# Both products of each rotation in the S5 scan on the vector engine, in a two-layer hybrid trunk on one Trainium2 core

## The chip, the core and the metric

The kernel runs on one core of one Trainium2 chip. The metric is device time in microseconds, from the first to the last instruction of one launch, of the median of the runs. Before the change it is 2625.96 us (three runs, 2624.56 to 2633.85 us). The engines are named as the profile names them: PE is the tensor engine (PEld its weight loads), DVE the vector engine, ACT the scalar engine, POOL is GpSimd, SP issues the weight loads.

## What is computed

Two layers of a decoder trunk for 256 tokens of width 2048. Layer 0 projects the normalised input once (2048 x 4632) and feeds two mixers, an S5 complex-diagonal state space (512 channels in 32 groups of 16, 64 complex states per group) and a Mamba-2 SSD mixer; layer 1 feeds an RWKV-7 mixer and an RG-LRU in the same manner. Each layer ends with an output projection, a squared-ReLU MLP (2048 to 8192 and back) and a gated embedding; a last RMSNorm ends the program. All is float32. The part that matters here is the scan of S5:

```python
bu_re = jnp.einsum('bsgh,gph->bsgp', ug, bbar_re)
bu_im = jnp.einsum('bsgh,gph->bsgp', ug, bbar_im)
def combine(e1, e2):
    a1r, a1i, b1r, b1i = e1
    a2r, a2i, b2r, b2i = e2
    return (a2r * a1r - a2i * a1i, a2r * a1i + a2i * a1r,
            a2r * b1r - a2i * b1i + b2r, a2r * b1i + a2i * b1r + b2i)
_, _, xr, xi = lax.associative_scan(combine, (a_re, a_im, bu_re, bu_im), axis=1)
y = einsum('ghp,bsgp->bsgh', c_re, xr) - einsum('ghp,bsgp->bsgh', c_im, xi)
```

## The kernel before

Weights stream from memory in tiles of 512 KB (128 x 1024 values, `raw`), three in flight. Each tile is split into a high part `wh` (an ACT copy, line 172) and a low part `wl` (a DVE subtraction, line 153), three buffers of each in layer 0, and PE makes three passes with them: `gemm_as` (lines 339 to 341, 512 columns at a time) and `gemm_ws` (lines 358 to 360, 256 columns). A tile feeds PE with 12 products of 512 columns or 24 of 256. So PE can't go on without the next `wl`, and neither ACT nor DVE can split further ahead than the three buffers that PE gives back.

Layer 0 (`even`) goes through a list of steps, `ORA`, in which S0 to S3 are the four tiles of S5 (`s5_tile`, 128 channels each), T the tables of cos and sin, U the loads of u, Z, C, B and X0 pieces of the big projection with their convolutions on DVE (line 166, `c<-fpad`), Q scores, and E the decays of the SSD mixer (`ssd_decays`, lines 843 to 876: softplus, sums by PE, exponentials, the transposes on line 868, and after them the exponents on lines 901 and 902). The list `ORB` follows with the SSD groups.

The complex recurrence is made real: the inputs are rotated by the angle of each state back to a common phase, two real scans run, and the result is rotated forth. One `s5_tile` holds four such pieces j of 32 channels. For each piece PE makes the two inputs (line 667) into PSUM, ACT copies them to SBUF as `b` (128 x 512), `s5_rotate` turns them (sign -1), DVE scans two chunks of 128 tokens with a carry between them (line 681, the carry `kar` by ACT and DVE), `s5_rotate` turns the states (sign 1), and PE multiplies them with C (line 685). So there are 4 x 4 x 2 = 32 rotations. A rotation has two products with broadcast tables, `p2` with sin and `p1` with cos, 128 x 512 each, and two sums of halves, 128 x 256 each. The helpers are `tt` (line 153, on `self.ve`, which is DVE here) and `gtt` (line 156, always POOL).

The program is written through a tile framework whose scheduler lays out one fixed order for each engine, from its own estimate of each instruction's cost. At run time each engine works through its own order and waits on semaphores for the others. High-priority parts (the weight splits) are put ahead where the scheduler can.

Of the kernel before, what the change touches and what calls it, by code (L numbers as in the profile page):

```python
# [15 lines left out]
OP = mybir.AluOpType  # L16
PSUM = bass.MemoryType.PSUM
# [6 lines left out]
S5C = 128  # L24
S5N = 16
# [31 lines left out]
# order of the steps of layer 0 (to the S5 part, and after it) and of layer 1; see even() and odd()  # L57
# [4 lines left out]
# steps that go first when their inputs are there, and steps of layer 0 whose weights are not split ahead  # L62
URGENT = ("G1", "Q")
LATE_W = ("L", "Pa01", "X0")
# steps of layer 1 whose weights are split ahead, and projections in column blocks of 256
EARLY_W = ("D2", "D3", "L00", "L01", "L10", "L11")
N256 = ("D0", "D3")
# column blocks of the embedding gate
# [3 lines left out]
class K:  # L72
# [20 lines left out]
    @contextmanager  # L93
    def on_pool(self, on=True):
        """Small elementwise work goes to GpSimd."""
        if on:
            self.ve = self.nc.gpsimd
        yield
        self.ve = self.nc.vector
# [4 lines left out]
    @contextmanager  # L104
    def phase(self, name, wp, **n):
        """Buffers of split weights and PSUM banks of a phase: accumulators, transposes, and others by tag."""
        with ExitStack() as st:
            if wp:
                self.wp = st.enter_context(self.weights(name, wp))
            self.ps = st.enter_context(self.tc.tile_pool(name="ps" + name, bufs=1, reuse_waits="tile", space=PSUM))  # L110
            self.nb = n
            yield
# [165 lines left out]
    def rsqrt_small(self, v, n):  # L278
        """Exponent halving, a fitted step (to 7e-4) and one of third order."""
        b = self.small(n, I32)  # L280
        self.ts(b, v.bitcast(I32), 1, None, OP.logical_shift_right)
        y = self.small(n)
        self.ts(y.bitcast(I32), b, -1.0, 1595932665.0, OP.mult, OP.add)
        w, q = self.small(n), self.small(n)
        k = 0.703952253 * 3 / 8
        self.tt(w, y, y, OP.mult)
        self.stt(w, w, -k, v, OP.mult, OP.mult)
        self.stt(y, w, 2.38924456 * k, y, OP.add, OP.mult)
        self.stt(w, y, 64.0 / 9, y, OP.mult, OP.mult)
        self.tt(w, w, v, OP.mult)  # L290
        self.stt(q, w, -10.0 / 3, w, OP.add, OP.mult)
        self.stt(y, q, 5.0, y, OP.add, OP.mult)
        return y

# [27 lines left out]
    def gemm_as(self, xs, W, r0, c0, nn=512, shared=False):  # L322
        """x times columns of W, tokens on partitions: an accumulator per 128 tokens, or both in one bank."""
        nk = len(xs)
        if shared:
            q = self.acc([128, 2, nn])
            ps = [q[:, 0], q[:, 1]]
        else:
            ps = [self.acc([128, nn]) for _ in range(2)]
        step = 2 * 512 // nn  # L330
        f = dict(skip_group_check=True)
        for kb in range(0, nk, step):
            wh, wl = self.wtile(W, r0[kb] if isinstance(r0, list) else r0 + kb, step, c0, nn)
            for kk in range(step):
                k = kb + kk
                h, l = xs[k]
                for t in range(2):
                    s = slice(128 * t, 128 * t + 128)
                    self.nc.tensor.matmul(ps[t], h[:, s], wh[:, kk], start=k == 0 and not (shared and t), stop=False, **f)  # L339
                    self.nc.tensor.matmul(ps[t], h[:, s], wl[:, kk], start=False, stop=False, **f)  # L340
                    self.nc.tensor.matmul(ps[t], l[:, s], wh[:, kk], start=False, stop=k == nk - 1, **f)  # L341
        return ps
# [21 lines left out]
    def prep(self, src, g, j0, nj, alloc=None):  # L364
        """src(t, j): [128 tokens, 128] of feature tile j; g(j): per-feature scale or None."""
        hb, lb = ((alloc or self.t4)([128, nj, T], FR) for _ in range(2))
        for i in range(nj):
            q = self.pq([128, T])
            for t in range(2):
                self.nc.tensor.transpose(q[:, 128 * t:128 * t + 128], src(t, j0 + i), self.ident)  # L370
            if g is None:
                self.split(hb[:, i], lb[:, i], q)
            else:
                s = g(j0 + i)
                self.pa = self.act(hb[:, i], q, AF.Copy, scale=s)
                self.pv = self.stt(lb[:, i], q, s, hb[:, i].bitcast(F32), OP.mult, OP.subtract)
                self.pas.append((self.pa, self.pv))
        return [(hb[:, i], lb[:, i]) for i in range(nj)]

    def norm_prep(self, gname):  # L380
        """Transposed, scaled and split h, and the reciprocal rms of each token."""
        xs = []
        ss = self.small(8)
        last = []
# [24 lines left out]
    def load_x(self, src, W, pool):  # L409
        """The input and the first weights, in the order of their use."""  # L410
        self.h = [[self.c([128, 1024], pool=pool) for _ in range(2)] for _ in range(2)]
        self.early = []
        for b in range(4):
            for t in range(2):
                self.nc.sync.dma_start(self.hv(t, 512 * b, 512), src[128 * t:128 * t + 128, 512 * b:512 * b + 512])
            if b < 3:
                self.early.append(self.wload(W, 2 * b, 2, 0, 512))
# [27 lines left out]
    def project_y(self, ys, W, **k):  # L445
        """Adds the product of channel-layout y with rows from 128 r of W, for pairs (y, r)."""
# [9 lines left out]
    def mlp(self, i, w1, w2, between):  # L456
        """relu(r x)^2 = r^2 relu(x)^2 for the reciprocal rms r > 0 of a token, which goes to the product's end."""
# [27 lines left out]
    def embed_prep(self, i, p, pool):  # L485
        """Transposed and split input embeddings."""
# [6 lines left out]
    def embed(self, i, px, W, Wg, out=None):  # L493
        with self.scope(f"embed{i}") as self.lp:
# [23 lines left out]
            if out is not None:  # L518
                # the last columns for the first 128 tokens, and then for the others
# [58 lines left out]
    def s5_start(self):  # L578
        """Tables for t < S5N, and cos, sin and -sin at S5N and its doubles."""
# [23 lines left out]
    def s5_tables(self, m):  # L603
        """cos and sin of t * angle for t < S5C, and at S5C."""
# [14 lines left out]
    def s5_split(self, u):  # L619
        """Splits B, and u by way of DRAM."""  # L620
# [9 lines left out]
    def s5_stack(self, m):  # L630
        """Channels 32 j .. 32 j + 31 of u's tile m: high, low, high and low parts, one below the other."""
# [5 lines left out]
    def s5_tile(self, m, u, us, e, w):  # L637
        """Channels 128 m .. 128 m + 127 (8 groups) of S5."""
# [52 lines left out]
    def s5_rotate(self, b, e, j, sign):  # L691
# [3 lines left out]
        self.gtt(p2, b, sb, OP.mult)  # L695
# [6 lines left out]
    def gelu(self, o, y, n):  # L702
        """y * 0.5 * (1 + tanh(sqrt(2/pi) (y + 0.044715 y^3)))"""
# [17 lines left out]
    def evac_rows(self, ps, i, n, pad, rows, w=128):  # L721
        """Scaled copy of channel-layout accumulators i and i + 1, with `pad` zeros before the first token."""
# [5 lines left out]
    def conv(self, o, f, i, w, b):  # L728
        """Causal width-4 convolution of tile i of f."""
# [110 lines left out]
    def ssd_decays(self, x):  # L840
# [32 lines left out]
        # 2^100 below the diagonal, to be taken from the exponents  # L873
# [88 lines left out]
    def shifted(self, o, ps, i0, rows, m0, w=128):  # L962
        """f + (f of the token before - f) * mu for tiles i0 and i0 + 1 of o"""
# [56 lines left out]
    def rwkv_in(self, xs, Wi, hf, c2, x, rows):  # L1020
        """Keys, receptances and values of two tiles."""
# [9 lines left out]
    def rwkv_consts(self):  # L1031
        nc = self.nc
        C = 64
        # mask over [beta | k] rows and [alpha | r] columns; the products of beta and alpha go elsewhere
# [11 lines left out]
        # takes the mean over a head's channels from its values, and so from its outputs  # L1046
# [7 lines left out]
        # partitions with an even and an odd share of 32-blocks  # L1054
# [3 lines left out]
        # rows of two heads, from the high and the low parts  # L1058
# [8 lines left out]
    def lora_up(self, W, lo, c0, i0, w, nk):  # L1067
        """Product of the low-rank activations with columns c0 .. c0 + 255 of W, in channel layout."""
# [13 lines left out]
    def rwkv_keys(self, hf, c2, lo, A, st):  # L1082
        """Decays, gains and unit keys of two tiles."""
# [16 lines left out]
        # unit keys  # L1100
# [27 lines left out]
    def rwkv_products(self, hf, c2, st):  # L1128
        """Products of keys and receptances within the chunks."""
# [7 lines left out]
        # centred values in token layout, on the second half of the partitions  # L1137
# [6 lines left out]
        for i in range(2):  # L1144
# [16 lines left out]
            # bonus, in place of v  # L1161
# [11 lines left out]
            g = []  # L1173
# [13 lines left out]
            # the decay of the chunk before goes to alpha and r, as it isn't in that chunk's state  # L1187
# [11 lines left out]
    def rwkv_inverse(self, hf, st):  # L1199
        nc = self.nc  # L1200
        lp = self.l
        # minus the transposed inverse of I + L, one 32-block per partition; of two partitions with the same block
        # (16 apart) the first takes the even rows and the second the odd ones
# [21 lines left out]
    def rwkv_chain(self, hf, st):  # L1225
        """States from chunk to chunk, of pairs of tiles; two heads' blocks on the diagonal of S."""
# [64 lines left out]
    def rwkv_post(self, hf, st):  # L1291
        """Head norm, bonus and gate, in place of the bonus."""
# [26 lines left out]
    def lru(self, i, j2, out, xs, rows, Wi, lam, A):  # L1319
# [32 lines left out]
        # 1 - exp(2 x) = -tanh(x) (1 + exp(2 x))  # L1352
# [19 lines left out]
    def final_start(self, gsrc):  # L1372
        """Weights of the last norm, and what is done with each block of columns of h that is complete."""
# [130 lines left out]
```

## Time and profile before

| what | us |
|---|---|
| median of the runs shown (lowest, highest) | 2625.96 (2624.56, 2633.85) |
| the profiled execution, span from first to last instruction | 2627.8 |
| PE busy in it | 2544.1 |
| DVE busy in it | 1640.6 |
| POOL busy in it | 180.3 |

The profile gives no time of its profiled execution other than the span, so the span stands for it. A busy time is the union of the intervals in which an engine has an instruction; instructions of one engine overlap a little at their ends, so the distance from one start to the next is shorter than a duration. An instruction that is held up while it runs shows a longer duration, not a wait. A wait is idle time of an engine before an instruction, put down to what ended it.

### The profile page before, as it was taken

Reading aid. Unit: us, or ns where it says so; the run is one execution under the profiler, and the core shown is the slowest. Engines: PE = TensorE matmul, PEld = TensorE weight load, DVE = VectorE, ACT = ScalarE, POOL = GpSimd, SP = SyncE. Lnnn points to the kernel's source line nnn. Section 1 sums busy time; section 2 is a strip of 40 time slices with the busy share of each in tenths; the row PEclk is TensorE's granted clock in tenths of the full one; section 3 lists DMA queues with packets and bytes.
Section 4 is the critical chain, followed back from the end, with each engine's and each line's share of the span. In section 5 each row is a group of like instructions: output and inputs, shape, how many; then the busy total and the mean of one; then the engine's idle time right before and its main releaser. Section 6 shows DMA issues by size and latency. Waiting matters only on the chain. (4 is left out here: it accounts for less than half of the span.)

```text
span 2627.8 us, 41133 instructions
## 1 busy us (share of the span) xinstructions
PE 2544.1 (97%) x16352; PEld 2287.2 (87%) x16352; DVE 1640.6 (62%) x2525; ACT 1301.5 (50%) x1886; POOL 180.3 (7%) x287
## 2 busy tenths in 40 slices
PE   7888999999999999999999999999999999999998
PEld 7776878989989988978899998889998899899787
DVE  7989786555555455466566688876545555555565
ACT  5353654544444444445455567546444444444464
POOL 4433110000000000000100010100000000000000
PEclk9999999999999999999999999999999999999999
DMA  6453335566665665655555533456666666665654
GB/s 201 135 137 112 111 118 184 169 185 185 186 187 186 182 188 184 185 184 183 177 162 164 151 102 108 137 168 194 192 185 186 185 185 187 187 185 178 191 179 142
DMA packets 262593, 443.27 MB, mean 169 GB/s; under 512 B 16768, under 2 KB 81408, under 8 KB 262400
## 3 DMA queue, kind: packets, MB, share of 16 engines
q1 hardware_dynamic: 256560, 431.25, 54.5%
q0 software_dynamic: 5696, 9.18, 1.2%
q8 instruction: 128, 2.10, 0.3%
q14 instruction: 65, 0.53, 0.1%
q10 hardware_dynamic: 144, 0.21, 0.0%
HBM read 435.34 MB, written 5.24 MB: 168 GB/s over the span
## 5 line engine op out<-in xcount | busy, mean ns | idle before, releaser
L153 DVE TENSOR_TENSOR wl<-raw,wh 128x1024 fp32r<-128x1024 f32 x810 | 992.7, 1226 | 811.7 <-ACT wh L172 811.4
L172 ACT ACTIVATE wh<-raw 128x1024 fp32r<-128x1024 f32 x811 | 856.0, 1056 | 1075.4 <-PE acc L341 527.7
L360 PE MATMUL acc<-t,wl 128*128 128x256 f32 x3136 | 895.7, 286 | 3.4 <-DVE wl L153 3.3
L358 PE MATMUL acc<-t,wh 128*128 128x256 f32 x3136 | 896.9, 286 | 1.1 <-ACT t L172 1.1
L359 PE MATMUL acc<-t,wh 128*128 128x256 f32 x3136 | 895.8, 286 | 0.0
L360 PEld LDWEIGHTS acc<-t,wl 128*128 128x128 f32 x3136 | 604.2, 193 | 6.9 <-DVE wl L153 5.2
L358 PEld LDWEIGHTS acc<-t,wh 128*128 128x128 f32 x3136 | 604.2, 193 | 3.6 <-ACT t L172 1.3
L359 PEld LDWEIGHTS acc<-t,wh 128*128 128x128 f32 x3136 | 604.4, 193 | 1.9 <-issue 0.3
L340 PE MATMUL acc<-wl,hid 128*128 128x512 f32 x1024 | 407.0, 398 | 0.0
L339 PE MATMUL acc<-wh,hid 128*128 128x512 f32 x1024 | 404.8, 395 | 0.0
L341 PE MATMUL acc<-wh,hid 128*128 128x512 f32 x1024 | 404.4, 395 | 0.0
L339 PEld LDWEIGHTS acc<-wh,hid 128*128 128x128 f32 x1024 | 192.4, 188 | 46.9
L341 PEld LDWEIGHTS acc<-wh,hid 128*128 128x128 f32 x1024 | 192.3, 188 | 45.4
L340 PEld LDWEIGHTS acc<-wl,hid 128*128 128x128 f32 x1024 | 192.3, 188 | 44.3
L340 PE MATMUL acc<-wl,t 128*128 128x512 f32 (+1 forms) x480 | 180.9, 377 | 1.3 <-DVE wl L153 1.3
L341 PE MATMUL acc<-wh,t 128*128 128x512 f32 (+1 forms) x480 | 179.9, 375 | 0.0
L339 PE MATMUL acc<-wh,t 128*128 128x512 f32 (+1 forms) x480 | 179.9, 375 | 0.0
L340 PEld LDWEIGHTS acc<-wl,t 128*128 128x128 f32 x480 | 92.1, 192 | 16.9 <-DVE wl L153 1.7
L341 PEld LDWEIGHTS acc<-wh,t 128*128 128x128 f32 x480 | 91.9, 192 | 14.8
L339 PEld LDWEIGHTS acc<-wh,t 128*128 128x128 f32 x480 | 91.7, 191 | 15.2
L340 PE MATMUL acc<-wl,xh 128*128 128x256 f32 (+1 forms) x224 | 75.2, 336 | 1.5 <-DVE wl L153 1.5
L339 PE MATMUL acc<-wh,xh 128*128 128x256 f32 (+1 forms) x224 | 76.3, 341 | 0.0
(343 smaller groups left out, 2222.5 us busy)
## 6 DMA issues: line engine op xcount, KB each, us to landing
raw<-in_mlp_w SPq DMA_DIRECT2D x512, 512.0 KB, 3.8
raw<-in_o_in_proj SPq DMA_DIRECT2D x84, 512.0 KB, 3.7
raw<-in_e_in_proj SPq DMA_DIRECT2D x72, 512.0 KB, 3.7
raw<-in_pl_gate SPq DMA_DIRECT2D x64, 512.0 KB, 3.9
raw<-in_e_out_proj SPq DMA_DIRECT2D x32, 512.0 KB, 3.6
raw<-in_o_out_proj SPq DMA_DIRECT2D x32, 512.0 KB, 3.6
raw<-in_pl_proj SPq DMA_DIRECT2D x8, 512.0 KB, 3.8
c<-in_x SPq DMA_DIRECT2D x8, 256.0 KB, 7.3
```

Of the source, the lines that this page charges most:

```text
L153: self.ve.tensor_tensor(o, a, b, op=op)
L172: return self.nc.scalar.activation(o, a, f, **k)
L339: self.nc.tensor.matmul(ps[t], h[:, s], wh[:, kk], start=k == 0 and not (shared and t), stop=False, **f)
L340: self.nc.tensor.matmul(ps[t], h[:, s], wl[:, kk], start=False, stop=False, **f)
L341: self.nc.tensor.matmul(ps[t], l[:, s], wh[:, kk], start=False, stop=k == nk - 1, **f)
L358: self.nc.tensor.matmul(out, wh[:, kk, o:o + mw], h, start=k == 0 and m % 2 == 0, stop=False, **f)
L359: self.nc.tensor.matmul(out, wh[:, kk, o:o + mw], l, start=False, stop=False, **f)
L360: self.nc.tensor.matmul(out, wl[:, kk, o:o + mw], h, start=False, stop=k == nk - 1, **f)
```

## The change

In `s5_rotate` the product with sin goes through `tt` in place of `gtt`. All else in the diff is comments and docstrings taken out, which leaves every line number as it was.

```diff
     def s5_rotate(self, b, e, j, sign):
         sh = [128, 2, T // S5C, S5C]
         cb, sb = (e[:, i:i + 1, j:j + 1].to_broadcast(sh) for i in range(2))
         p1, p2 = self.l("s5t", 10, sh), self.l("s5t", 10, sh)
-        self.gtt(p2, b, sb, OP.mult)
+        self.tt(p2, b, sb, OP.mult)
         self.tt(p1, b, cb, OP.mult)
         o = (OP.add, OP.subtract)
         self.tt(p1[:, 0], p1[:, 0], p2[:, 1], o[sign > 0])
         self.tt(p1[:, 1], p1[:, 1], p2[:, 0], o[sign < 0])
```

The scheduler lays the orders out anew. Here is DVE in the second tile of S5, before, from the carry of one piece to the scan of the next (`s5t_1200` and `s5t_1228` are the states of two pieces that follow each other, `s5t_1215` the first one's rotated states, `tab` the tables):

```order
L166 SCALAR_TENSOR_TENSOR kar_1209<-s5t_1200,tw2_722,kar_1208 128x1 x2
L681 SCALAR_TENSOR_TENSOR s5t_1200<-c15_364,kar_1209,s5t_1200 128x128 x2
L153 TENSOR_TENSOR wl_1868<-raw_1865,wh_1867 128x1024
L153 TENSOR_TENSOR s5t_1215<-s5t_1200,tab_803 128x512
L153 TENSOR_TENSOR s5t_1228<-s5t_1226,tab_803 128x512
L153 TENSOR_TENSOR s5t_1215<-s5t_1215,s5t_1216 128x256 x2
L153 TENSOR_TENSOR wl_1886<-raw_1883,wh_1885 128x1024
L153 TENSOR_TENSOR s5t_1228<-s5t_1228,s5t_1229 128x256 x2
L681 SCALAR_TENSOR_TENSOR s5t_1228<-c15_364,s5t_1228 128x128 x2
```

And the same place with the change:

```order
L166 SCALAR_TENSOR_TENSOR kar_1209<-s5t_1200,tw2_722,kar_1208 128x1 x2
L681 SCALAR_TENSOR_TENSOR s5t_1200<-c15_364,kar_1209,s5t_1200 128x128 x2
L153 TENSOR_TENSOR wl_1886<-raw_1883,wh_1885 128x1024
L153 TENSOR_TENSOR s5t_1216<-s5t_1200,tab_803 128x512
L153 TENSOR_TENSOR s5t_1215<-s5t_1200,tab_803 128x512
L153 TENSOR_TENSOR s5t_1229<-s5t_1226,tab_803 128x512
L153 TENSOR_TENSOR s5t_1215<-s5t_1215,s5t_1216 128x256 x2
L153 TENSOR_TENSOR s5t_1228<-s5t_1226,tab_803 128x512
L166 SCALAR_TENSOR_TENSOR c20_1307<-fpad_1550,c2_77,c20_1307 128x256
L153 TENSOR_TENSOR s5t_1228<-s5t_1228,s5t_1229 128x256 x2
L681 SCALAR_TENSOR_TENSOR s5t_1228<-c15_364,s5t_1228 128x128 x2
```

The products `s5t_1216` and `s5t_1229`, which were POOL's, stand in DVE's order, the second of them ahead of the first piece's sums. Next is DVE behind the last rotation of S5, before (`s5t_2334`; `y5` and `ga` are the S5 output and its GeLU, `c26_2817` the step sizes and `c28_2851` the summed decays of step E, which PE sums from `c27_2846`):

```order
L153 TENSOR_TENSOR s5t_2334<-s5t_2334,s5t_2335 128x256 x2
L153 TENSOR_TENSOR wl_3111<-raw_3108,wh_3110 128x1024
L166 SCALAR_TENSOR_TENSOR y5_2342<-u_401,c2_77,pm_2229 128x256
L166 SCALAR_TENSOR_TENSOR c25_2350<-fpad_2606,c2_77,c25_2350 128x256
L854 COPY c28_2851<-pm_2848 128x48
L166 SCALAR_TENSOR_TENSOR ga_2344<-ga_2344,y5_2342 128x256
```

And with the change:

```order
L153 TENSOR_TENSOR s5t_2334<-s5t_2334,s5t_2335 128x256 x2
L166 SCALAR_TENSOR_TENSOR c25_2350<-fpad_2606,c2_77,c25_2350 128x256
L153 TENSOR_TENSOR wl_3171<-raw_3168,wh_3170 128x1024
L166 SCALAR_TENSOR_TENSOR y5_2342<-u_401,c2_77,pm_2229 128x256
L166 SCALAR_TENSOR_TENSOR c25_2350<-fpad_2606,c2_77,c25_2350 128x256
L845 COPY c26_2817<-sm_2806 128x48
L166 SCALAR_TENSOR_TENSOR c25_2350<-fpad_2606,c2_77,c25_2350 128x256
L166 SCALAR_TENSOR_TENSOR ga_2344<-ga_2344,y5_2342 128x256
L166 SCALAR_TENSOR_TENSOR c27_2846<-c26_2817,sm_2827 128x48
L854 COPY c28_2851<-pm_2848 128x48
```

The weight split behind the last rotation is of a later tile (`wl_3171` in place of `wl_3111`, two tiles on), and the end of the softplus of step E, which stood far ahead of S5's end before, stands behind it.

## Rows read from the trace of the kernel before

**Rows 1.** The page: span, and busy time of the engines.

```profile
span 2627.8 us, 41133 instructions
PE 2544.1 (97%) x16352; PEld 2287.2 (87%) x16352; DVE 1640.6 (62%) x2525; ACT 1301.5 (50%) x1886; POOL 180.3 (7%) x287
```

**Rows 2.** Windows of the run; columns in the first line, clock as share of full speed.

```profile
core 0: us, PE busy (x) PEld busy (x) DVE busy (x) ACT busy (x) POOL busy (x), PEclk, DMA share, GB/s
75.00:275.00 200.00, 162.58 (x999) 144.79 (x999) 182.24 (x345) 85.21 (x146) 74.52 (x56) 0.95 0.46 128
275.00:400.00 125.00, 119.12 (x718) 100.56 (x717) 95.42 (x174) 77.35 (x146) 16.77 (x15) 0.97 0.38 116
```

**Rows 3.** Waits of PE, 55 to 280 us: total us, times, longest us.

```profile
PE pm L685 <- DVE s5t L153: 33.1, 16, 4.8
```

**Rows 4.** Waits of DVE, 55 to 280 us.

```profile
DVE wl L153 <- ACT wh L172: 15.8, 12, 5.0
DVE s5t L153 <- POOL s5t L156: 5.8, 5, 1.2
DVE s5t L153 <- POOL fpad L724: 2.4, 2, 1.2
```

**Rows 5.** DVE's groups, 75 to 275 us: busy us, mean ns, idle before.

```profile
L153 DVE TENSOR_TENSOR wl<-raw,wh 128x1024 fp32r<-128x1024 f32 x47 | 59.7, 1270 | 8.1 <-ACT wh L172 8.0
L153 DVE TENSOR_TENSOR s5t<-s5t 128x256 f32<-128x256 f32 x64 | 35.0, 581 | 8.3 <-POOL s5t L156 5.8 <-POOL fpad L724 2.4
L153 DVE TENSOR_TENSOR s5t<-s5t,tab 128x512 f32<-128x512 f32 x32 | 30.8, 980 | 0.1
```

**Rows 6.** DVE in order of time, no product on POOL: start us, us, instruction.

```profile
83.55 0.69 DVE L153 TENSOR_TENSOR s5t<-s5t,tab 128x512 f32<-128x512 f32 x1
84.15 1.22 DVE L153 TENSOR_TENSOR wl<-raw,wh 128x1024 fp32r<-128x1024 f32 x1
85.29 0.49 DVE L153 TENSOR_TENSOR ttmp<-tab,tw 128x128 f32<-128x128 f32 x2
85.69 0.42 DVE L153 TENSOR_TENSOR s5t<-s5t 128x256 f32<-128x256 f32 x1
```

**Rows 7.** POOL's group of rotation products, and one with DVE idle, in order of time.

```profile
L156 POOL TENSOR_TENSOR s5t<-s5t,tab 128x512 f32<-128x512 f32 x32 | 63.2, 1989 | 112.0 <-DVE s5t L681 101.2 <-ACT s5t L172 10.8
...
188.82 1.30 POOL L156 TENSOR_TENSOR s5t<-s5t,tab 128x512 f32<-128x512 f32 x1 [3.82 <-ACT s5t L172]
```

**Rows 8.** POOL, DVE and PE in order of time, around one rotation.

```profile
117.40 4.26 POOL L156 TENSOR_TENSOR s5t<-s5t,tab 128x512 f32<-128x512 f32 x2 [3.97 <-DVE s5t L681]
117.48 0.69 DVE L153 TENSOR_TENSOR s5t<-s5t,tab 128x512 f32<-128x512 f32 x1
118.09 1.22 DVE L153 TENSOR_TENSOR wl<-raw,wh 128x1024 fp32r<-128x1024 f32 x1
120.48 1.80 DVE L153 TENSOR_TENSOR s5t<-s5t 128x256 f32<-128x256 f32 x2 [1.17 <-POOL s5t L156]
122.00 1.13 PE L685 MATMUL pm<-s5t,bd 128*128 128x256 f32 x4 [2.16 <-DVE s5t L153]
```

**Rows 9.** PE, DVE and ACT in order of time, last rotation of S5 and what follows.

```profile
274.18 0.70 PE L685 MATMUL pm<-s5t,bd 128*128 128x256 f32 x2 [1.44 <-DVE s5t L153]
275.91 0.47 DVE L166 SCALAR_TENSOR_TENSOR c<-fpad,c,c 128x256 f32<-128x256 f32 x1
276.30 0.19 DVE L854 COPY c<-pm 128x48 f32<-128x48 f32 x1
276.45 1.28 ACT L172 ACT_TABLE_LOAD   x1
280.76 0.28 PE L358 MATMUL acc<-t,wh 128*128 128x256 f32 x1
280.88 0.28 PE L359 MATMUL acc<-t,wh 128*128 128x256 f32 x1
286.52 0.38 PE L868 MATMUL pq<-c,c 128*48 128x128 f32 x2
```

## The prediction

> **What bounds the kernel now.** The page comes first: PE is busy for 2544.1 of 2627.8 us [rows 1], so for most of the run only PE's own work counts, and work on DVE or POOL is free or nearly so. The change touches one stretch, so the next view is the windows. From 75 to 275 us, where the 32 rotations lie, PE is busy for only 162.6 of 200 us and DVE for 182.2; in the next 125 us PE is at 119.1 and DVE at 95.4 [rows 2]. So the S5 stretch is the one place where DVE is the fuller engine. The waits say who waits for whom there: PE stands 33.1 us, in 16 waits of about 2 us, before the products of line 685, each time for DVE's sum at the end of a forward rotation [rows 3]. DVE itself waits for POOL's products 5.8 us, for a small POOL instruction queued behind them (`fpad`) 2.4 us, and for ACT's `wh` 15.8 us [rows 4], of which 8.0 lie behind 75 us [rows 5]. So DVE sets the pace of this stretch: what it gains or loses there, PE gains or loses, and behind it PE is nearly full to the end.
>
> Next, what DVE's time is made of. Alone, a 128x512 product takes 0.69 us and the next instruction starts 0.60 us after it (83.55 to 84.15); a 128x256 sum takes 0.42, a `wl` split 1.22, with 1.14 to the next start [rows 6]. In the stretch the same forms have means of 0.980, 0.581 and 1.270 us [rows 5]. One rotation shows why: POOL starts two products at 117.40, DVE does its own product and a split at their usual length, then waits 1.17 us for POOL, and the two sums that should take some 0.8 us take 1.80, while POOL makes its second product [rows 8]. The two engines hold each other up, and PE, which waits for the first sum, starts at 122.00 after 2.16 us of idleness. POOL's product takes 1.30 us when DVE is idle and 1.99 in the mean [rows 7].
>
> **What the change removes and adds.** I count DVE's instructions up to its sums for the last product on line 685, at 274.18 us [rows 9], in both orders.
>
> Added: 32 products at 0.60 us from start to start [rows 6], 19.2 us. They have the shape, types and table pattern of the 32 that DVE makes already, so the duration is known. The new order also has two more `wl` splits ahead of that point (63 for 61, 2 x 1.14 = 2.3 us), one convolution step less (0.39 us from 275.91 to 276.30 [rows 9]) and two small instructions less (some 0.3 us). In all DVE has 19.2 + 2.3 - 0.7 = 20.8 us more to do.
>
> Removed: what POOL's products cost DVE. From the means less the lone durations [rows 5, 6]: 32 products x (0.980 - 0.69) = 9.3 us; 64 sums x (0.581 - 0.42) = 10.3; 47 splits x (1.270 - 1.22) = 2.3; and the waits, 5.8 + 2.4 = 8.2 [rows 4]. Together 30.1 us, 0.94 per rotation. POOL's own 63.2 us go too [rows 7], but nothing waits for POOL's being busy other than what was just counted; with the products gone its queue holds only clears, small copies and DMA issues there.
>
> The Trainium skill (SBUF — State Buffer, section on the two separate sides) says that a vector instruction with two SBUF inputs and a GpSimd instruction that reads SBUF share one port pair, that whichever starts first holds it for its whole length, and that the other blocks. The sums in rows 8 agree, the split beside POOL's first product, at its usual 1.22 us, agrees too if DVE had the port and POOL stood still. By that rule each product would cost DVE its lone length, and the time would be 32 x 1.30 - 30.1 = 11.5 us shorter than by my sum (an estimate by that page); I stay with what the rows add up to.
>
> So the last product on line 685 comes 30.1 - 20.8 = 9.3 us earlier. PE has more behind it by then: in its new order 46 more products of 256 columns stand ahead of that point than before (895 for 849, with as many of 512), which at 0.12 us from start to start (280.76 to 280.88 [rows 9]) is 5.5 us of PE work that no longer follows. PE is nearly full from there on [rows 2], so both count: 9.3 + 5.5 = **14.8 us less**.
>
> Unknown costs, each with both ends. (1) DVE's waits for `wh`, 8.0 us in the stretch [rows 5]. They depend on when PE gives buffers back; they could go (-8.0), or, as PE and DVE are both nearer to full, double (+8.0). I leave them as they are. (2) What POOL cost DVE: at most 32 x 1.30 = 41.6 us, if each product blocked DVE for its lone length [rows 7], 11.5 more than counted; at least the waits and the sums, 8.2 + 10.3 = 18.5, if the rest were something else, 11.6 less. The counted 30.1 is a sum of measured differences, so I take that. (3) The moved end of step E. Its sums on PE now stand 23 products behind line 685's last, and the transposes on line 868 another 51 behind them, 51 x 0.12 = 6.1 us. From the copy `c<-pm` to line 868 the trace has 10.2 us (276.30 to 286.52), without a wait of PE [rows 9]; if all of it were needed, PE would wait 4 us. But three table loads of 1.28 us like the one shown lie on ACT's way there, and the new ACT order has one. So 0 to 4 us, and I take 0. (4) In the new order a product of the next piece sometimes stands ahead of the sums that PE waits for; it costs 0.60 us at such a rotation and is in DVE's count already.
>
> What hides the 20.8 us is not PE, which waits for DVE at every rotation, but the time that POOL's products take from DVE now; if less of it comes back than that, the rest is on the path.
>
> **The sum.** Against the profiled execution 2627.8 - 14.8 = 2613.0; that span is 1.8 us above the median of the runs, and against the median, which is what will be compared, 2625.96 - 14.8 = **2611 us**. A measurement of this kernel tells 0.5%, 13.1 us, from no change, so the border is 2612.8, close to the forecast.
>
> **The rivals.**
> - *More comes back.* The waits for `wh` go with the stalls of PE (-8.0), or POOL's hold cost more than the sum shows. For it: PE's 16 waits [rows 3] and its clock of 0.95 [rows 2], which leave room. Against: DVE still has more work than PE between any two rotations. 2611 - 8 = 2603, 0.20.
> - *Two full engines wait for each other.* From the first line-685 product to the last, PE's new order holds 671 products of 256 columns where it held 550, 121 x 0.12 = 14.5 us more, with DVE's work there larger as well. DVE's waits for `wh` double, or step E's end makes PE wait: 8 to 12 us of the gain are gone. 2621, 0.20.
> - *Slower.* DVE is the full engine, at 182.2 of 200 us [rows 2], and gets 20.8 us more. If its long rows are not POOL's doing but come from elsewhere, they stay, and the time is 20.8 - 5.5 = 15.3 us longer: 2641. It decides where less than 15.3 us of the 30.1 come back, 0.48 per rotation. For it: POOL's products have hidden 63.2 us [rows 7] off DVE. Against: the same forms at their short length wherever POOL makes no product [rows 6]. 0.08. The Trainium skill (Perfetto Trace Analysis, section on optimizing scalar and DVE operations) speaks for this one: with DVE saturated, offloading to GpSimd may make sense; it adds that between these two it might not help, for the shared port, and rows 8 show that it does not.
> - *Nothing moves.* The orders exclude it: POOL's list has lost all 32 products and DVE's has them. 0.
>
> **How the numbers follow.** Forecast 0.50 (its own range 2604 to 2618), more 0.20, mutual waits 0.20, slower 0.08, other 0.02. Below 2612.8 lie the second case and some six tenths of the first: 0.50. Over 2639 lie the slower case and a part of the rest: 0.09. Between: 0.41. The range goes from 2600, which leaves out the far end of the second case, to 2623, which takes in the third and leaves out the slower one.
>
> **What would show it.** In the new profile POOL should have no `s5t<-s5t,tab` group. On DVE that group should count 64 at 0.69 us, the 64 sums should be at 0.42 to 0.43 us, and the waits for POOL should be gone. The last product on line 685 should start near 274.2 - 9.3 = 265 us, and line 868 near 272, that is 286.5 - 14.8. PE's waits before line 685 should shrink from 33.1 us by some 15 to 20. Wrong it would be if the sums stay long (the slower case), if DVE shows new waits for `wh` or for ACT's copies of 8 us and more, or if PE waits on line 868.

## The result, and the profile after

The changed kernel takes 2600.11 us (median of four runs, 2598.30 to 2603.81), the kernel before 2628.82 us in the four runs beside them (2624.56 to 2633.85). The ratio is 0.9883, with a 95% interval of 0.9868 to 0.9898: 1.17%, or some 30 us, less. The forecast was 14.8 us less. The direction was right; the forecast size was about half of what came, and the time lies at the very end of the stated range, 2600 to 2623 us.

The page of the profiled execution, span and busy times, answers to [rows 1]:

```profile
span 2597.7 us, 41093 instructions
PE 2538.0 (98%) x16352; PEld 2284.7 (88%) x16352; DVE 1630.8 (63%) x2557; ACT 1301.1 (50%) x1885; POOL 119.6 (5%) x255
```

The span is 30.1 us shorter, and DVE, which got 32 products more, is busy for 9.8 us less in the whole run. The groups of DVE from 55 to 275 us say how; they answer to [rows 5] (busy us, mean ns of one, idle before):

```profile
L153 DVE TENSOR_TENSOR wl<-raw,wh 128x1024 fp32r<-128x1024 f32 x55 | 67.0, 1220 | 9.8 <-ACT wh L172 9.8
L153 DVE TENSOR_TENSOR s5t<-s5t,tab 128x512 f32<-128x512 f32 x64 | 41.9, 687 | 0.0
L153 DVE TENSOR_TENSOR s5t<-s5t 128x256 f32<-128x256 f32 x64 | 24.5, 421 | 0.0
```

The mean product fell from 980 to 687 ns, the sum from 581 to 421, the split from 1270 to 1220: all three stand at the lengths that [rows 6] show where POOL makes no product. The 64 products together take 41.9 us where 32 took 30.8. No wait for POOL is left among them. DVE's waits for `wh` are shorter too, which the first row from 75 to 275 us, the window of [rows 5], shows at 3.1 us where it had 8.0:

```profile
L153 DVE TENSOR_TENSOR wl<-raw,wh 128x1024 fp32r<-128x1024 f32 x53 | 64.4, 1216 | 3.1 <-ACT wh L172 3.1
```

One rotation of the new order, DVE in order of time, beside [rows 8]:

```profile
119.81 0.69 DVE L153 TENSOR_TENSOR s5t<-s5t,tab 128x512 f32<-128x512 f32 x1
120.41 1.22 DVE L153 TENSOR_TENSOR wl<-raw,wh 128x1024 fp32r<-128x1024 f32 x1
121.55 1.29 DVE L153 TENSOR_TENSOR s5t<-s5t,tab 128x512 f32<-128x512 f32 x2
122.75 0.76 DVE L153 TENSOR_TENSOR s5t<-s5t 128x256 f32<-128x256 f32 x2
123.42 1.22 DVE L153 TENSOR_TENSOR wl<-raw,wh 128x1024 fp32r<-128x1024 f32 x1
```

The row of two sums takes 0.76 us, where it took 1.80 behind a wait of 1.17. PE's waits from 55 to 256 us follow; the first row of [rows 3] is now the third, at a tenth of what it was:

```profile
PE acc L360 <- DVE wl L153: 8.2, 3, 5.0
PE pm L833 <- ACT d L172: 4.6, 1, 4.6
PE pm L685 <- DVE s5t L153: 3.4, 9, 0.6
```

Where the 30.1 us lie in the run is read from PE at three places. These are the last products on line 685, the transposes on line 868 and the last group of the SSD scores on line 928. Before, the first two stand in [rows 9], at 274.18 and 286.52 us, and the third is this row of PE in order of time:

```profile
377.62 1.45 PE L928 MATMUL pm<-xd,dec 128*128 128x64 f32 x12
```

All three after:

```profile
255.16 1.13 PE L685 MATMUL pm<-s5t,bd 128*128 128x256 f32 x4 [0.23 <-DVE s5t L153]
264.59 0.38 PE L868 MATMUL pq<-c,c 128*48 128x128 f32 x2
347.46 1.45 PE L928 MATMUL pm<-xd,dec 128*128 128x64 f32 x12
```

So 19.0 us are gained up to the last product of S5, 21.9 up to step E's transposes, 30.2 up to the end of the SSD scores, and nothing behind them. The two parts, by windows. Kernel before, from 60 us to the start of its last sums, and from its last product on line 685 to the end of line 928:

```profile
core 0: us, PE busy (x) PEld busy (x) DVE busy (x) ACT busy (x) POOL busy (x), PEclk, DMA share, GB/s
60.00:273.71 213.71, 175.72 (x1046) 154.72 (x1046) 194.26 (x366) 90.14 (x153) 88.82 (x79) 0.94 0.48 132
274.18:379.07 104.89, 101.10 (x637) 86.35 (x638) 78.11 (x138) 68.25 (x133) 11.41 (x11) 0.97 0.34 103
```

The same two stretches after:

```profile
60.00:254.67 194.67, 178.10 (x1088) 159.31 (x1088) 188.07 (x396) 92.81 (x156) 29.09 (x47) 0.94 0.54 149
255.16:348.91 93.75, 92.38 (x595) 78.77 (x596) 74.00 (x139) 65.08 (x130) 10.34 (x11) 1.00 0.34 107
```

In the first stretch, 19.0 us shorter, DVE is busy for 6.2 us less and idle for 6.6 us in place of 19.5. In the second, 11.1 us shorter, PE has 42 matmuls less, is idle for 1.4 us in place of 3.8, and has its full clock (1.00, that is 2.4 GHz) where it had 0.97.

### The profile page after: what moved, and what is told of

Its sections match the earlier page's. It is cut to its first block, busy times and chain, and to the rows that moved or that the text cites. A ratio compares the mean times of both kernels' runs of the same rounds, so it can differ in the third digit from the quotient of the medians.

```text
span 2597.7 us, 41093 instructions
## 1 busy us (share of the span) xinstructions
PE 2538.0 (98%) x16352; PEld 2284.7 (88%) x16352; DVE 1630.8 (63%) x2557; ACT 1301.1 (50%) x1885; POOL 119.6 (5%) x255
## 5 line engine op out<-in xcount | busy, mean ns | idle before, releaser
L341 PEld LDWEIGHTS acc<-wh,t 128*128 128x128 f32 x480 | 91.5, 191 | 14.7
```

## The experiments

The theory: a POOL instruction that reads SBUF holds DVE, whoever uses its result, so what the change brings is the end of that hold. Rivals: only the forward products matter, since PE stands behind them; the gain comes from the new order; DVE should be relieved further, not loaded; POOL's being busy is enough to slow DVE. Ratios are to the kernel before, run beside each (its medians lay from 2628.82 to 2633.10 us), with the 95% interval.

| run | us | ratio |
|---|---|---|
| the change | 2600.11 | 0.9883 [0.9868, 0.9898] |
| e3: 32 idle products on POOL | 2642.18 | 1.0051 [1.0034, 1.0069] |
| e4: 32 idle products on DVE | 2629.53 | 0.9998 [0.9988, 1.0007] |
| e5: 64 clears of scratch on POOL | 2604.11 | 0.9905 [0.9883, 0.9926] |
| e11: 64 clears of `b` on POOL | 2599.31 | 0.9884 [0.9863, 0.9906] |
| e12: 32 copies of `b` on POOL | 2614.94 | 0.9938 [0.9919, 0.9957] |
| e1: forward half of the change | 2611.99 | 0.9935 [0.9915, 0.9955] |
| e2: backward half | 2609.63 | 0.9924 [0.9905, 0.9944] |
| e6: both products on POOL | 2655.11 | 1.0096 [1.0081, 1.0111] |
| e7: no sine products | 2588.55 | 0.9843 [0.9828, 0.9858] |
| e8: SSD groups on DVE too | 2603.28 | 0.9901 [0.9884, 0.9917] |
| e9: first tables on DVE too | 2602.52 | 0.9891 [0.9874, 0.9909] |
| e10: all tables on DVE | 2597.65 | 0.9875 [0.9860, 0.9890] |

### Is it the hold? The products put back on POOL, with nobody reading them

```diff
         self.tt(p2, b, sb, OP.mult)
+        self.gtt(self.l("dum", 1, sh, mybir.dt.bfloat16), b, sb, OP.mult)
```

> The changed kernel, and POOL makes the 32 sine products once more, into a scratch tile that nobody reads; the orders of PE, DVE and ACT are those of the changed kernel, row for row. Theory A (a product on POOL that reads SBUF takes DVE's time, whoever uses its result): the sums go back to long durations or DVE idles, some 0.9 us for each product, up to 1.3; the time rises by 20 to 40 us to about 2620 to 2640, with DVE's own added products now on top. Theory B (the gain came from the new order, and from DVE and PE no longer waiting for POOL's results): nothing waits for the scratch tile, so 2600, within 5 us.

It is slower than the kernel before, by 0.51%, and 1.7% (some 44 us) over the changed kernel, 2 us beyond the range of theory A. PE, DVE and ACT work through the same orders as in the changed kernel, and no instruction reads the scratch tile, so the difference between these two kernels comes neither from an order of theirs nor from a wait for a product's value. DVE's groups from 55 to 330 us:

```profile
L153 DVE TENSOR_TENSOR wl<-raw,wh 128x1024 fp32r<-128x1024 f32 x58 | 78.2, 1349 | 19.0 <-ACT wh L172 19.0
L153 DVE TENSOR_TENSOR s5t<-s5t,tab 128x512 f32<-128x512 f32 x64 | 52.1, 844 | 0.0
L153 DVE TENSOR_TENSOR s5t<-s5t 128x256 f32<-128x256 f32 x64 | 27.6, 466 | 0.0
L166 DVE SCALAR_TENSOR_TENSOR c<-fpad,c,c 128x256 f32<-128x256 f32 x36 | 19.9, 577 | 0.6 <-ACT c L172 0.6
```

All four forms are longer than in the changed kernel, the convolution too, which has nothing to do with S5. One case in order of time, POOL and then DVE:

```profile
173.71 1.28 POOL L156 TENSOR_TENSOR dum<-s5t,tab 128x512 bf16<-128x512 f32 x1 [1.64 <-DVE s5t L681]
174.14 1.13 DVE L166 SCALAR_TENSOR_TENSOR c<-fpad,c,c 128x256 f32<-128x256 f32 x1 [0.58 <-ACT c L172]
175.19 1.28 DVE L153 TENSOR_TENSOR s5t<-s5t,tab 128x512 f32<-128x512 f32 x2
```

POOL's product runs from 173.71 to 174.99; the convolution, usually 0.47 us, starts inside it and ends at 175.27, 0.28 us after it; the two products behind it are of their usual length again. The window from 60 us to the last sums, to be laid beside the changed kernel's first one above, and then the stretch behind line 685's last:

```profile
60.00:302.04 242.04, 192.79 (x1088) 170.93 (x1088) 220.07 (x397) 94.05 (x157) 101.24 (x83) 0.87 0.41 120
302.50:396.27 93.77, 92.41 (x595) 78.81 (x596) 73.98 (x139) 64.82 (x130) 10.27 (x11) 1.00 0.33 107
```

DVE is busy for 220.07 us in place of 188.07: 32.0 us, 1.00 us for each product that POOL makes. The stretch is 47.4 us longer, not 32.0: DVE is idle for 22.0 us too, in place of 6.6. PE, for the same 1088 matmuls, is busy for 14.7 us more, at a clock of 0.87 in place of 0.94. Behind it, the 93.75 us of the changed kernel come back as 93.77. This profiled execution is the longest of the run's seven; the median lies 10 us under it, and 5.8 us of what it has over the changed kernel's profile lie behind line 928, where all is as in the changed kernel.

The 47.4 us contain something besides the longer instructions and what follows from them. POOL also clears the tiles `bd` (line 642), which ACT then fills for the products of S5, and these clears now stand behind the scratch products in POOL's queue. ACT's waits for them from 60 us to the last sums, here and in the changed kernel:

```profile
ACT bd L172 <- POOL bd L642: 21.0, 6, 6.2
ACT bd L172 <- POOL bd L642: 4.8, 6, 1.8
```

The kernel before had 4.1 us of them. So DVE's 32.0 us are the hold, as they are the length of its instructions; how much of the other 15.4 us is POOL's lateness, and how much follows from the hold, is not separated.

### The same idle products on DVE

```diff
         self.tt(p2, b, sb, OP.mult)
+        self.tt(self.l("dum", 1, sh, mybir.dt.bfloat16), b, sb, OP.mult)
```

> The changed kernel with the 32 sine products made once more on DVE, into a scratch tile that nobody reads: 19.2 us more of DVE's work in the S5 stretch, and none on POOL. If DVE's time there passes one to one to the end: 2600 + 19 = 2619. If waits between DVE and PE make more of it, as in the run with scratch products on POOL (32.7 us more of DVE's busy time, 42 us more at the end, 1.3 to one): 2625. If DVE has room left after the change: 2600 to 2610.

1.16% (30 us) over the changed kernel, for some 20 us of work on DVE, and more than any of the three expectations (whose 32.7 us of DVE for e3 are 31.7 by the two pages, 1662.5 and 1630.8); still some 14 us better than the same work on POOL. Here the scheduler made a new order, with one PE wait of 13.6 us in it (55 to 300 us):

```profile
PE acc L360 <- DVE wl L153: 13.9, 2, 13.6
PE pm L685 <- DVE s5t L153: 9.0, 8, 3.8
```

So a microsecond added to DVE came with more than one at the end here, but how much of that is the order's is not separated.

### What must POOL do to hold DVE? Clears and copies

First clears of a scratch tile:

```diff
         self.tt(p2, b, sb, OP.mult)
+        d = self.l("dum", 1, sh, mybir.dt.bfloat16); self.nc.gpsimd.memset(d, 0.0); self.nc.gpsimd.memset(d, 0.0)
```

> The changed kernel with two clears of a 128x512 tile on POOL per rotation, which read nothing, in place of the scratch products; the orders of PE, DVE and ACT are again those of the changed kernel. If only POOL instructions that read SBUF hold DVE up, the time is that of the changed kernel, 2600 within 4 us, and DVE's sums stay at 0.42 us. If any work on POOL does, it lies near the run with scratch products, over 2615.

This one missed its aim. The clears depended on nothing, so all 64 had started by 62.1 us, ahead of the rotations, and only made POOL's tables late. The time says nothing on the hold. So the clears were tied to `b`, the rotation's input, which has just been used up:

```diff
         self.tt(p1, b, cb, OP.mult)
+        self.nc.gpsimd.memset(b, 0.0); self.nc.gpsimd.memset(b, 0.0)
```

> The changed kernel, and GpSimd clears the rotation's used-up input b twice per rotation (64 clears of 128x256 float32, which stand inside the S5 stretch since b has to be read first); the clears read nothing. If only work that reads two SBUF tiles holds VectorE (the theory): 2600 +- 4 us, sums at 0.42 us and products at 0.69, as in the changed kernel. If any GpSimd work beside VectorE holds it: at the price per instruction of the 32 idle products (1.02 us) halved for the size, 64 x 0.5 = 33 us of VectorE, so above 2620 us, with sums nearer to 0.47.

The time is the changed kernel's. POOL's clears from 55 to 275 us, and DVE's products and sums beside them:

```profile
L696 POOL MEMSET s5t<- 128x512 f32 x64 | 33.7, 526 | 127.1 <-DVE s5t L153 111.6 <-ACT wh L172 5.4 <-DVE sm L160 4.0
L153 DVE TENSOR_TENSOR s5t<-s5t,tab 128x512 f32<-128x512 f32 x64 | 41.9, 687 | 0.0
L153 DVE TENSOR_TENSOR s5t<-s5t 128x256 f32<-128x256 f32 x64 | 24.5, 420 | 0.0
```

33.7 us of POOL's writing inside the stretch change nothing in these forms of DVE: 687 and 420 ns. Keeping POOL busy for that long, and `b` in use, costs nothing either. (The clears are 128 x 512; the expectation named half of that, and priced them so. At the full size its rival price would have been twice as high.) Then a copy, which reads one tile:

```diff
         self.tt(p1, b, cb, OP.mult)
+        self.nc.gpsimd.tensor_copy(self.l("dum", 1, sh, mybir.dt.bfloat16), b)
```

> The changed kernel, and one GpSimd copy of the rotation's used-up input b (one SBUF tile read) into a bfloat16 scratch tile per rotation, 32 in all, which nobody reads. If it is the second input that makes the hold: 2600 +- 4 us with sums at 0.42. If reading one tile holds VectorE as two do: 32 x 1.02 = 33 us of VectorE, up to the 2642 us of the idle products. If in proportion to what is read: half of that, about 2615 to 2625 us.

0.56% (14 us) over the changed kernel, at the foot of the range "in proportion to what is read": reading one tile holds DVE too, for less. The copies and DVE's groups, 55 to 275 us, and the window to the last sums:

```profile
L695 POOL CAST dum<-s5t 128x512 bf16<-128x512 f32 x32 | 47.3, 1477 | 120.6 <-DVE s5t L681 87.4 <-DVE sm L166 22.6 <-ACT s5t L172 10.1
L153 DVE TENSOR_TENSOR s5t<-s5t,tab 128x512 f32<-128x512 f32 x64 | 45.5, 741 | 0.0
L153 DVE TENSOR_TENSOR s5t<-s5t 128x256 f32<-128x256 f32 x64 | 25.9, 440 | 0.0
```

```profile
60.00:265.70 205.70, 178.79 (x1088) 158.67 (x1088) 199.44 (x397) 93.37 (x156) 72.25 (x79) 0.95 0.50 141
```

DVE is busy for 11.4 us more, 0.36 us for each copy. Here the stretch is 11.0 us longer, one to one, and PE's clock and DVE's idle time (6.3 us) are as in the changed kernel; another 5.6 us of this execution lie behind line 928, as in e3. The hold goes both ways; two rows of POOL from the same kernel:

```profile
155.55 0.61 POOL L695 CAST dum<-s5t 128x512 bf16<-128x512 f32 x1 [2.46 <-DVE s5t L681]
188.71 7.30 POOL L695 CAST dum<-s5t 128x512 bf16<-128x512 f32 x2 [7.58 <-DVE s5t L681]
```

A copy that takes 0.61 us by itself takes 3.6 us each in the second row: there POOL is the one that stands.

For VectorE instructions with two SBUF inputs, the Trainium skill (SBUF — State Buffer, section on the two separate sides) limits its rule to GpSimd instructions that read SBUF. The three runs agree on GpSimd's side, as clears hold nothing and copies and products do. The Trainium skill says in the same place that the hold lasts for the whole instruction. Measured are 1.00 us of a product that takes 1.28 alone and 0.36 of a copy that takes 0.61, in the mean. That some of POOL's instructions stand still themselves, as in the second row above, would fit; how many do was not counted.

### Which half of the change brings it

Only the forward products moved, and only the backward ones:

```diff
-        self.tt(p2, b, sb, OP.mult)
+        (self.tt if sign > 0 else self.gtt)(p2, b, sb, OP.mult)
```

```diff
-        self.tt(p2, b, sb, OP.mult)
+        (self.tt if sign < 0 else self.gtt)(p2, b, sb, OP.mult)
```

> Only the forward rotation (sign 1, the one that PE waits for) has both products on DVE; the backward one keeps its sine product on POOL. Theory A: half of the products, half of the change in time: about 2614 (2609 to 2619). Theory B: the forward rotation is the one that ends PE's waits before line 685, so nearly all of the gain: 2600 to 2606.

> Only the backward rotation (sign -1) has both products on DVE. Theory A: about half of the change, 2614 (2609 to 2619). Theory B: PE still waits for POOL's product at each forward rotation, so little gain, 2622 to 2629.

The forward half alone brings 0.65%, the backward half 0.76%, the whole 1.17%. PE waits for the forward sums only, and the backward half, on which it does not wait, is worth no less. So the theory that PE's place behind the forward products decides falls. By the ratios either half alone brings more than half. But both intervals reach half of the change (0.9941), and each half has an order of its own, so it is not shown that the first piece of hold that goes is worth more than the second. In e2 the forward products are still POOL's, and DVE's sums, at their short length, wait 10.4 us for them (55 to 330 us):

```profile
L153 DVE TENSOR_TENSOR s5t<-s5t 128x256 f32<-128x256 f32 x64 | 24.3, 419 | 12.7 <-POOL s5t L156 10.4 <-POOL fpad L724 2.3
```

### The other ends: both products on POOL, and no sine products

```diff
-        self.gtt(p2, b, sb, OP.mult)
-        self.tt(p1, b, cb, OP.mult)
+        self.gtt(p2, b, sb, OP.mult)
+        self.gtt(p1, b, cb, OP.mult)
```

(against the kernel before), and against the changed kernel:

```diff
-        self.tt(p2, b, sb, OP.mult)
...
-        self.tt(p1[:, 0], p1[:, 0], p2[:, 1], o[sign > 0])
-        self.tt(p1[:, 1], p1[:, 1], p2[:, 0], o[sign < 0])
+        self.tt(p1[:, 0], p1[:, 0], b[:, 1], o[sign > 0])
+        self.tt(p1[:, 1], p1[:, 1], b[:, 0], o[sign < 0])
```

> The kernel before with both products of each rotation on POOL: 64 products there, DVE freed of 32 (19.2 us). Theory A (each product on POOL takes about 1 us from DVE): 32 x (1.0 - 0.6) = 13 us more for DVE and the sums wait for two products in a row; 2640 to 2670. Rival (DVE is the full engine, so what leaves it helps): 2610 or less.

> The changed kernel without the sine products on any engine (the sums read the rotation's input in their place, so each rotation computes something else): DVE has 19.2 us less to do in the stretch. If DVE still sets the pace: 2585 to 2590. If PE is the bound by now, its waits before line 685 being 3.4 us in all: 2593 to 2600.

With both products on POOL, DVE has 32 instructions less than before and the kernel is 0.96% slower. Its splits and its sums, 55 to 330 us:

```profile
L153 DVE TENSOR_TENSOR wl<-raw,wh 128x1024 fp32r<-128x1024 f32 x54 | 76.0, 1408 | 27.1 <-ACT wh L172 26.8 <-issue 0.3
L153 DVE TENSOR_TENSOR s5t<-s5t 128x256 f32<-128x256 f32 x64 | 48.1, 798 | 16.5 <-POOL s5t L156 16.5
```

And PE's waits for the sums, 55 to 320 us:

```profile
PE pm L685 <- DVE s5t L153: 41.1, 26, 5.2
```

The Trainium skill (Perfetto Trace Analysis, section on optimizing scalar and DVE operations) names offloading to GpSimd for a saturated DVE and warns that the shared port may spoil it. These runs, at 2655, 2629 and 2600 us with 64, 32 and no products on POOL, show the warning to be the part that holds here.

Without the sine products, DVE has 19.2 us less to do than in the changed kernel, and the time falls by 0.40%, 10 us: about half of it, inside the range that was given for DVE still setting the pace. This kernel has an order of its own as well. That DVE sets only part of the pace by now is a reading of this window: it is busy for 169.23 of 172.11 us there and PE for 165.43, so PE has nearly no room left to give.

```profile
60.00:232.11 172.11, 165.43 (x1036) 147.03 (x1036) 169.23 (x367) 89.22 (x153) 24.11 (x47) 0.98 0.59 162
```

### Can more be had?

Ten elementwise steps of the SSD groups moved from POOL to DVE as well (lines 941 and 946); the tables of the first S5 tile (line 766); and these with the start of all tables (line 756).

```diff
-                self.gtt(yt[:, t], yo, yt[:, t], OP.add)
+                self.tt(yt[:, t], yo, yt[:, t], OP.add)
...
-                self.gtt(ys, ys, sz[n][:, :, a - 512 * n:b - 512 * n], OP.mult)
+                self.tt(ys, ys, sz[n][:, :, a - 512 * n:b - 512 * n], OP.mult)
```

```diff
-                            with self.on_pool(m == 0), self.tc.issue_after(self.ra.ins):
+                            with self.on_pool(False), self.tc.issue_after(self.ra.ins):
```

```diff
-                with self.on_pool(), self.tc.issue_after(self.ra.ins):
+                with self.on_pool(False), self.tc.issue_after(self.ra.ins):
```

> The changed kernel with the ten sums and products of the SSD groups (lines that write yg on POOL, 15.3 us there) on DVE too. Theory A: each takes from DVE about as long as it is on POOL alone (1.0 to 1.9 us), and costs 0.5 to 0.9 us on DVE; the stretch from 261 to 386 us has PE at 121.5 of 125, so little shows: 2594 to 2600. Rival (DVE's added work makes PE wait): 2603 or more.

> The changed kernel with the tables of the first S5 tile (six products and six sums, 8.0 us on POOL) on DVE as well. Theory A: they hold DVE up for about as long now, and cost DVE 4 to 5 us; a gain of 2 to 6 us, 2594 to 2599. Rival: they stand where DVE waits for other things, and the tables come no earlier: 2600 within 3 us.

> As the run before, and the start of the tables (a serial chain of small instructions, about 20 us on POOL from 38 to 58 us) on DVE as well. Theory A alone would say faster again; but DVE is busy there with the first weight splits, and the chain would stand between them: 2595 to 2615, slower than the run before if PE waits for splits in the first 60 us.

None can be told from the changed kernel: the three intervals overlap the change's. The gains that theory A gave for e8 and e9 did not show; their medians, 2603.28 and 2602.52 us, are where the rivals had them. The last has the lowest median, 2597.65 us, inside its wide range.

## Why the prediction was wrong in size

**What bounds.** Right. DVE's time in the S5 stretch set the pace, and PE's waits on line 685 were DVE's. They shrank from 33.1 us to 3.4, more than the 15 to 20 that were forecast.

**Added: 19.2 us of products.** Right: 64 at 687 ns.

**Removed: "Together 30.1 us, 0.94 per rotation".** Too small. Of these 30.1 us, 8.2 are waits for POOL and 21.9 are long rows. The waits are gone, as counted. But DVE's busy time up to the last sums fell by 6.2 us (194.26 to 188.07), although some 20.8 us of work came in, so the long rows had cost some 27.0 us (an estimate: 6.2 + 20.8). That makes 35.2 in all, still inside the bounds of 18.5 to 41.6 that unknown (2) gave. The busy time that e3 puts back, 32.0 us, is to be laid beside the 21.9 and the 27.0, as nothing there waits for a product's value.

**"So the last product on line 685 comes 30.1 - 20.8 = 9.3 us earlier."** This is the step that failed. It came 19.0 us earlier, and the windows of the two kernels say where the missing 9.7 us are. By the prediction's terms DVE's busy time should have fallen by 1.1 us (20.8 added, 21.9 of long rows gone) and its idle time by the 8.2 us of waits for POOL; they fell by 6.2 and 12.9. So 5.1 us are the long rows, counted too low, and 4.7 are other idle time: the waits for `wh`, of which the prediction said "I leave them as they are", went from 8.0 to 3.1 us.

Why the waits for `wh` shrank is not shown. e3 and e12, with the orders of the changed kernel, show that a microsecond of DVE is not always one of the stretch: in the profiled executions 11.4 us more of DVE make it 11.0 us longer, 32.0 us more make it 47.4 longer. In e3 PE stands, its granted clock is 0.87, the same matmuls take it 14.7 us more, and DVE and ACT wait more; ACT also waits for POOL's `bd` there. That these go together is measured; which of them starts the rest was not separated. By the ratios of the runs e12 costs 14 us for 11.4 and e3 44 for 32.0, that is 1.2 and 1.4, so the steep price is in part the one long execution. That the kernel before lay on such a steep part is a guess: its waits for `bd` were 4.1 us, not 21.0.

e3 is near to the prediction's slower rival, the hold staying while DVE makes all the products, for which the forecast was 15.3 us over the kernel before; measured were 0.51%, 13 us. That they are so close is partly luck. In the profiled execution the stretch up to the last sums was 28.3 us longer than before, not 20.8, and the one behind it 11.1 us shorter, not 5.5.

**"46 more products ... 5.5 us" behind it.** Too small: the stretch behind line 685 is 11.1 us shorter. In the records 42 matmuls are gone, which at the prediction's 0.12 us is 5.0; PE waits 2.4 us less; the rest, 3.7 us, is PE's busy time, the clock having gone from 0.97 to 1.00. e3 repeats the stretch at 93.77 us with the hold in place ahead of it, so this part belongs to the new order and not to the hold. With the 9.7 us above, the 5.6 us that were missing here make up the 15.3 us between the forecast and the 30.1 us of the profiles. The 42 matmuls stand ahead of it now (1088 for 1046 in the first stretch), and the 19.0 us were gained with them inside.

**Unknown (3), step E.** Right at 0: PE does not wait on line 868 after. But it came at 264.59, not near 272.

**Unknown (1), `wh`.** Nearer to the favourable end: from 8.0 us behind 75 us to 3.1. The rival "more comes back" named both things that came, the waits for `wh` and a hold that costs more than the sum shows, with 2603 us, and the result lies 3 us beyond it. "Two full engines wait for each other" did not come with the change; such waits are seen in e3, e4 and e6, where DVE has more to do or to wait for.

**The aside on the port.** By the estimate that the prediction took from the Trainium skill (SBUF — State Buffer, section on the two separate sides), 32 x 1.30 us, the time would have been 2599.5 us. Measured were 2600.11. In part that is chance: the long rows and the waits came to some 35.2 us, not 41.6, and the rest came from the waits for `wh` and from the stretch behind line 685, which the estimate does not touch.

## What to carry to other kernels

Before work is moved from DVE to GpSimd, compare DVE's rows beside GpSimd's instructions with the same forms elsewhere: here a 1.3 us product that read SBUF took 0.8 to 1.0 us from DVE (27.0 and 32.0 us for 32 of them), which makes the same product itself in 0.6. Clears may stay there. And where two engines that feed each other are both nearly full, don't price a lost or gained microsecond at one without a look at whether the engine behind also waits, and at which clock; keep a steeper price (here 1.2 to 1.4 by the ratios) as an end of the range. A hold that is summed up from a few forms of instruction is a lower bound: here 21.9 us were counted where some 27 were gone. And work on a third engine delays whatever stands behind it in that engine's queue, as POOL's clears of `bd` in e3.

## What was not expected of the hardware

That POOL's writing costs DVE nothing and one input is enough: 64 clears of 128 x 512, 33.7 us of POOL beside the rotations, left DVE's forms at 687 and 420 ns, while 32 copies of one tile took 11.4 us from it. That a held stretch can grow by more than the hold: 47.4 us for 32.0, with PE's clock at 0.87, in an execution that is long for its run and has late clears of `bd` in it, while a hold of 11.4 us passed through at 11.0 with the clock at 0.95. And that idle work on POOL, which nobody reads, makes the kernel slower than the same work made by DVE, the engine that is fuller in the stretch: 2642 against 2630 us, the second in an order of its own.
